# 272 further matmuls at the end of a two-layer decoder step

## The chip, the cores and the metric

The kernel runs on one core of a Trainium2 chip. The metric is the device time of the core in microseconds (us); the median of the runs counts. A profiled execution has a time of its own beside its span, which runs from the first to the last instruction that the profiler recorded. TensorE multiplies matrices (a weight load, then a matmul that streams columns past the weights), VectorE (DVE), ScalarE (ACT) and GpSimd (POOL) do the rest, and SyncE (SP) starts most transfers.

## The reference

The kernel computes one inference step of a hybrid causal decoder trunk with two layers, for 272 prompt tokens (16 of them learned) and 64 tokens of eight decoding sequences, 336 in all, 2048 channels wide. Cut to what matters here:

```python
def mixer_layer(x, ...):
    h = rms_norm(x, norm_g)
    z = h @ w_in                       # 2048 -> 8 * 2048
    u, pg, q, k, v, rg, gp, gr = jnp.split(z, IN_OFFSETS, axis=-1)
    ...
    merged = jax.nn.sigmoid(gp) * pool_branch + jax.nn.sigmoid(gr) * ret_branch
    return x + merged @ w_out, new_hist, S_new
...
y_prompt = rms_norm(xp, final_norm)[:, N_META:]
y_sample = rms_norm(xs, final_norm)
```

Nothing of this is changed. The further matmuls multiply parts of a table of cosines and sines that the kernel holds anyway, and no output depends on them.

## The kernel before

Channels lie on the partitions and tokens along the free axis, so each activation is a row of 16 tiles of 128 channels by 336 tokens (320 in the second layer from its output side on, where the 16 learned tokens are no longer needed). All weights pass through one stream of steps. A step loads a block of 512 by 256 weights (`dma_step`), splits it into a high and a low part in float32r (`split_step`, L159 on ScalarE and L165 on VectorE) and runs 24 matmuls on it (`main_step`): for each of four k-slices and two halves of 128 output channels, high by high, high by low and low by high, each with a weight load of 128 columns of its own. Every matmul of the kernel but the transposes goes through the helper `mm`, line 155, so rows of L155 are told apart by their tiles and widths. Work between the steps (retention, pooling, gates) hangs on step numbers (`at`) and uses four PSUM buffers of 512 columns in turn (`side`).

The program order is written out by hand: what stands later in the program comes later on its engine. After the last step, two small groups of matmuls make the token sums and spread the resulting scale over the partitions (`token_sums`, `spread_rstd`). VectorE scales the eight parts of the result (L880) with that scale, read from the PSUM buffer `last`, and each part is sent out as soon as it is scaled, by SyncE's queue and ScalarE's in turn (L881):

```python
    for i in range(8):
        xf = H["xf", i]
        nc.vector.tensor_tensor(out=xf[:, :, n], in0=xf[:, :, n], in1=bc(last[:, n]), op=ALU.mult)
        (nc.sync, nc.scalar)[i % 2].dma_start(out=o["yT"][i], in_=xf[:, :, n])
```

Then the pools are closed. Line 925 (the call that runs the program) stands for the drains and the semaphores of the common end.

Of the kernel before, what the change touches and what calls it, by code (L numbers as in the profile page):

```python
# [6 lines left out]
F32 = mybir.dt.float32  # L7
F32R = mybir.dt.float32r
# [26 lines left out]
C_ID, C_COS, C_SIN = 0, 128, 128 + T  # L35
# [42 lines left out]
def build(tc, a, o, g8):  # L78
    nc = tc.nc
# [23 lines left out]
    def open_pool(name, side=None, **kw):  # L103
        P[name] = tc.alloc_tile_pool(name=name, bufs=1, side=side, reuse_waits="tile", **kw)
        return P[name]

    def close_pool(name):
        P.pop(name).release()

    def bc(ap, n=2):  # L110
        return ap.unsqueeze(1).to_broadcast([128, n, ap.shape[-1]])
# [9 lines left out]
    def side():  # L121
        return sidep.tile([128, 512], F32, tag="side", bufs=4, name="side")
# [4 lines left out]
    cst = cp.tile([128, C_W], F32, name="cst")  # L127
# [26 lines left out]
    def mm(out, lhsT, rhs, start, stop):  # L154
        nc.tensor.matmul(out, lhsT, rhs, start=start, stop=stop)  # L155
# [722 lines left out]
    for i in range(8):  # L878
        xf = H["xf", i]
        nc.vector.tensor_tensor(out=xf[:, :, n], in0=xf[:, :, n], in1=bc(last[:, n]), op=ALU.mult)  # L880
        (nc.sync, nc.scalar)[i % 2].dma_start(out=o["yT"][i], in_=xf[:, :, n])  # L881
    for name in list(P)[::-1]:
        close_pool(name)

# [52 lines left out]
```

## Time and profile before

| what | value |
|---|---|
| median of two runs | 2845.77 us (2845.53 to 2846.01) |
| profiled execution, its own time | 2847.05 us |
| its span | 2845.3 us |
| mean granted clock of TensorE over the span | 0.997 |
| TensorE busy | 2821.2 us, 99% of the span |
| VectorE, ScalarE, GpSimd busy | 53%, 33%, 13% |

Busy time of TensorE comes from modelled ends of overlapping matmuls: the time from one matmul's start to the next one's start is shorter than the duration that a row gives, and it is the first that adds up to a stretch. The clock column tells the share of full speed that TensorE was granted: 1.00 is 2.4 GHz, 0.50 is 1.2 GHz.

### The profile page before, as it was taken

Reading aid. Unit: us, or ns where it says so; the run is one execution under the profiler, and the core shown is the slowest. Engines: PE = TensorE matmul, PEld = TensorE weight load, DVE = VectorE, ACT = ScalarE, POOL = GpSimd, SP = SyncE. Lnnn points to the kernel's source line nnn. Section 1 sums busy time; section 2 is a strip of 40 time slices with the busy share of each in tenths; the row PEclk is TensorE's granted clock in tenths of the full one; section 3 lists DMA queues with packets and bytes.
Section 4 is the critical chain, followed back from the end, with each engine's and each line's share of the span. In section 5 each row is a group of like instructions: output and inputs, shape, how many; then the busy total and the mean of one; then the engine's idle time right before and its main releaser. Section 6 shows DMA issues by size and latency. Waiting matters only on the chain.

```text
span 2845.3 us, 46391 instructions
## 1 busy us (share of the span) xinstructions
PE 2821.2 (99%) x19228; PEld 2796.1 (98%) x19228; DVE 1518.4 (53%) x1898; ACT 932.8 (33%) x1117; POOL 362.4 (13%) x560
## 2 busy tenths in 40 slices
PE   8999999999999999999999999999999999999997
PEld 8999999999999999999999999999999999999997
DVE  7655555544345664344455566655544465644543
ACT  4333333333223333333333333333342333333332
POOL 5222222210000000000112222222100000000000
PEclk9999999999999999999999999999999999999998
DMA  6556565654554444444555666666655544444443
GB/s 240 189 205 214 205 212 201 219 194 165 166 179 140 148 150 144 153 153 164 195 187 204 212 209 210 210 214 219 212 167 172 174 153 159 143 156 162 172 167 122
DMA packets 174259, 516.63 MB, mean 182 GB/s; under 512 B 23888, under 2 KB 46672, under 8 KB 174032
## 3 DMA queue, kind: packets, MB, share of 16 engines
q1 hardware_dynamic: 150976, 447.81, 46.2%
q0 software_dynamic: 21696, 63.99, 6.3%
q8 instruction: 150, 2.46, 0.3%
q10 hardware_dynamic: 1376, 1.87, 0.2%
q14 instruction: 61, 0.50, 0.1%
HBM read 447.91 MB, written 66.57 MB: 181 GB/s over the span
## 4 chain that ended last, share of the span: by engine, by line
PE 98%; issue 0%; DVE 0%; POOL 0%; POOLq 0%; ACT 0%; DVEq 0%; ACTq 0%
PE acc L155 91%; PE side L155 6%; PE side L314 1%; PE side L485 0%; DVE xf L880 0%; DVE h_lo L167 0%; POOLq L925 0%; POOL xsq L215 0%; POOL xsq L214 0%; DVE xs L780 0%; ACT sq L208 0%; DVEq L925 0%; DVE sinr L236 0%; POOLq L214 0%; ACTq L208 0%
## 5 line engine op out<-in xcount | busy, mean ns | idle before, releaser
L155 PE MATMUL acc<-act_hi,whi 128*128 128x320 f32 (+1 forms) x3328 | 1039.7, 312 | 0.0
L155 PE MATMUL acc<-act_lo,whi 128*128 128x320 f32 (+1 forms) x3328 | 1037.4, 312 | 0.0
L155 PE MATMUL acc<-act_hi,wlo 128*128 128x320 f32 (+1 forms) x3328 | 1036.3, 311 | 0.0
L165 DVE TENSOR_TENSOR wlo<-raw,whi 128x1024 fp32r<-128x1024 f32 x720 | 868.7, 1226 | 293.1 <-ACT whi L159 285.4
L159 ACT CAST whi<-raw 128x1024 fp32r<-128x1024 f32 x720 | 733.6, 1047 | 511.2 <-PE acc L155 406.6
L155 PE MATMUL acc<-h_lo,whi 128*128 128x336 f32 x2304 | 732.9, 318 | 5.0 <-DVE h_lo L167 5.0
L155 PE MATMUL acc<-h_hi,whi 128*128 128x336 f32 x2304 | 736.1, 319 | 1.4 <-ACT whi L159 1.4
L155 PE MATMUL acc<-h_hi,wlo 128*128 128x336 f32 x2304 | 730.5, 317 | 0.7 <-DVE wlo L165 0.7
L155 PEld LDWEIGHTS acc<-act_lo,whi 128*128 128x128 f32 x3328 | 626.5, 188 | 0.0
L155 PEld LDWEIGHTS acc<-act_hi,wlo 128*128 128x128 f32 x3328 | 625.1, 188 | 0.0
L155 PEld LDWEIGHTS acc<-act_hi,whi 128*128 128x128 f32 x3328 | 624.8, 188 | 0.0
L155 PEld LDWEIGHTS acc<-h_lo,whi 128*128 128x128 f32 x2304 | 436.6, 190 | 7.6 <-DVE h_lo L167 7.5
L155 PEld LDWEIGHTS acc<-h_hi,whi 128*128 128x128 f32 x2304 | 433.6, 188 | 1.6 <-ACT whi L159 1.6
L155 PEld LDWEIGHTS acc<-h_hi,wlo 128*128 128x128 f32 x2304 | 434.1, 188 | 1.0 <-DVE wlo L165 1.0
L418 DVE SCALAR_TENSOR_TENSOR sraw<-sraw,side 128x512 f32<-128x512 f32 x128 | 87.9, 686 | 175.5 <-PE side L155 175.5
L419 POOL DMA_DIRECT2D out_ret_s_dram<-sraw x128 | 71.4, 558 | 524.4 <-DVE sraw L418 518.3
L212 POOL TENSOR_TENSOR xsq<-sq 128x336 f32<-128x336 f32 (+1 forms) x3 | 2.8, 941 | 564.8 <-ACT sq L208 564.8
L161 ACT ACTIVATE kthi<-side,cst 128x256 fp32r<-128x256 f32 (+1 forms) x48 | 20.9, 468 | 136.6 <-PE side L314 136.6
L669 POOL DMA_DIRECT2D out_pool_u_dram<-uc x16 | 8.7, 545 | 440.5 <-DVE uc L624 440.5
L159 ACT CAST vthi<-side 128x256 fp32r<-128x256 f32 (+1 forms) x48 | 16.2, 371 | 146.2 <-PE side L314 146.2
L582 DVE SCALAR_TENSOR_TENSOR mb<-tr,acc 128x336 f32<-128x336 f32 (+1 forms) x32 | 14.4, 493 | 81.0 <-PE acc L155 81.0
L389 DVE TENSOR_TENSOR sc<-side,dtab 128x416 f32<-128x416 f32 (+1 forms) x16 | 9.3, 583 | 90.3 <-PE side L155 90.3
(152 smaller groups left out, 1862.1 us busy)
## 6 DMA issues: line engine op xcount, KB each, us to landing
raw<-in_w_in_dram SPq DMA_DIRECT2D x512, 512.0 KB, 4.3
sraw<-in_state_ret_dram SPq DMA_DIRECT2D x128, 256.0 KB, 4.2
out_ret_s_dram<-sraw POOLq DMA_DIRECT2D x128, 256.0 KB, 2.6
raw<-in_proj_ret_dram SPq DMA_DIRECT2D x64, 512.0 KB, 4.1
raw<-in_proj_pool_dram SPq DMA_DIRECT2D x64, 512.0 KB, 5.0
raw<-in_w_out_dram SPq DMA_DIRECT2D x64, 512.0 KB, 4.8
raw<-in_pool_w_dram SPq DMA_DIRECT2D x16, 512.0 KB, 3.3
kts<-ktd SPq DMA_DIRECT2D x16, 256.0 KB, 3.0
```

Of the source, the lines that this page charges most:

```text
L155: nc.tensor.matmul(out, lhsT, rhs, start=start, stop=stop)
L159: nc.scalar.copy(out=out, in_=in_)
L161: nc.scalar.activation(out=out, in_=in_, func=ACTF.Copy, scale=scale)
L165: nc.vector.tensor_tensor(out=out, in0=in_, in1=hi.bitcast(F32), op=ALU.subtract)
L212: eng.tensor_tensor(out=xsq[:, n], in0=sq[:, 0, n], in1=sq[:, 1, n], op=ALU.add)
L314: nc.tensor.transpose(ps[:rows, 128 * d:128 * d + 128], hs[src][:, d, 128 * b:128 * b + rows], ident)
L389: nc.vector.tensor_tensor(out=sc[:, w], in0=ps[:, w], in1=dtab[:, w], op=ALU.mult)
L418: nc.vector.scalar_tensor_tensor(out=s2, in0=s2, scalar=g8[h], in1=up, op0=ALU.mult, op1=ALU.add)
L419: nc.gpsimd.dma_start(out=o["ret_s"][l, b, h].rearrange("p (d e) -> p d e", d=2), in_=s)
L582: nc.vector.scalar_tensor_tensor(out=t[:, d, n], in0=H["tr", l, i][:, d, n], scalar=1.0, in1=acc[:, d, n], op0=ALU.add, op1=ALU.mult)
L669: nc.gpsimd.dma_start(out=o["pool_u"][l, 2 * g + i], in_=gs.pop(("uc", i)))
```

## The change

Behind the eight output transfers, a pool of its own holds a tile of 640 float32r columns (`p_m`) and one of 256 (`p_w`), both copied by ScalarE from the constants. Then TensorE runs 272 matmuls in groups of 8 (the first group has 16), each with its weight load, into four PSUM buffers, two in a row into the same one. Widths are 512 (16 + 8), 320 (64), 336 (64 + 56), 448, 384, 304, 312, 328 and 344 (8 each), and 320 with only 64 or 32 weight columns (8 each). The 320 and 336 wide ones step the start of the moving operand by 8 elements (32 bytes) from 0 to 56, and a series of 336 steps the start of the weights by the same amounts.

```diff
         (nc.sync, nc.scalar)[i % 2].dma_start(out=o["yT"][i], in_=xf[:, :, n])
+    pr = open_pool("probe", side="left")
+    pad = pr.tile([128, 8], F32, name="pad")
+    p_m = pr.tile([128, 640], F32R, name="p_m")
+    p_w = pr.tile([128, 256], F32R, name="p_w")
+    nc.gpsimd.memset(pad, 0.0)
+    nc.scalar.copy(out=p_m, in_=cst[:, C_COS:C_COS + 640])
+    nc.scalar.copy(out=p_w, in_=cst[:, C_COS:C_COS + 256])
+    ps = [side() for _ in range(4)]
+
+    def probe(cols, off=0, woff=0, wide=128, count=8):
+        for i in range(count):
+            mm(ps[i // 2 % 4][:wide, :cols], p_w[:, woff:woff + wide], p_m[:, off:off + cols], True, True)
+
+    probe(512, count=16)
+    for cols in (320, 336):
+        for off in range(0, 64, 8):
+            probe(cols, off)
+    for woff in range(8, 64, 8):
+        probe(336, 0, woff)
+    for cols in (512, 448, 384, 304, 312, 328, 344):
+        probe(cols)
+    for wide in (64, 32):
+        probe(320, wide=wide)
     for name in list(P)[::-1]:
         close_pool(name)
```

## Rows read from the trace of the kernel before

**Rows 1.** The page: engines' busy time, and shares of the chain that ended last.

```profile
PE 2821.2 (99%) x19228; PEld 2796.1 (98%) x19228; DVE 1518.4 (53%) x1898; ACT 932.8 (33%) x1117; POOL 362.4 (13%) x560
...
PE acc L155 91%; PE side L155 6%; PE side L314 1%; PE side L485 0%; DVE xf L880 0%; DVE h_lo L167 0%; POOLq L925 0%; POOL xsq L215 0%; POOL xsq L214 0%; DVE xs L780 0%; ACT sq L208 0%; DVEq L925 0%; DVE sinr L236 0%; POOLq L214 0%; ACTq L208 0%
```

**Rows 2.** Timeline of the last 20 us: start, us, engine, line, operation, tiles.

```profile
2826.33 0.30 PE L155 MATMUL acc<-act_hi,wlo 128*128 128x320 f32 x1
...
2832.53 0.69 PE L155 MATMUL side<-cst,cosr 64*128 64x64 f32 x2
...
2833.26 5.94 DVE L880 TENSOR_TENSOR xf<-xf,side 128x640 f32<-128x640 f32 x8 [1.74 <-PE side L155]
...
2834.84 4.93 ACTq L881 DMA_DIRECT2D out_yT_dram<-xf  x4
```

**Rows 3.** What SyncE waited for in the last 25 us: us, times, longest.

```profile
SPq L925 <- DMA out_yT_dram<-xf: 4.8, 2, 3.5
```

**Rows 4.** The end's own instructions on line 925: durations in ns, first and last start.

```profile
L925 SPq DRAIN  x3: 7/7/7, 2844.4 to 2844.8; - x3
...
L925 PEldq DRAIN  x2: 13/856/1698, 2831.6 to 2844.8; - x2
```

**Rows 5.** Busy time by stretch at the end: engines, granted clock, DMA share, GB/s.

```profile
2830.00:2830.50 0.50, 0.00 (x0) 0.00 (x0) 0.04 (x1) 0.00 (x0) 0.39 (x1) 1.00 0.00 0
2830.50:2831.00 0.50, 0.00 (x0) 0.00 (x0) 0.00 (x0) 0.00 (x0) 0.50 (x1) 0.56 0.00 0
...
2843.50:2844.00 0.50, 0.00 (x0) 0.00 (x0) 0.00 (x0) 0.00 (x0) 0.00 (x0) 0.50 0.00 0
```

**Rows 6.** ScalarE: one instruction of the timeline, two groups of the page.

```profile
2813.57 0.74 ACT L208 ACTIVATE sq<-xs 128x640 f32<-128x640 f32 x1 [6.99 <-DVE xs L780]
L159 ACT CAST whi<-raw 128x1024 fp32r<-128x1024 f32 x720 | 733.6, 1047 | 511.2 <-PE acc L155 406.6
L159 ACT CAST vthi<-side 128x256 fp32r<-128x256 f32 (+1 forms) x48 | 16.2, 371 | 146.2 <-PE side L314 146.2
```

**Rows 7.** TensorE's timeline in steady work, second layer, 320 columns.

```profile
2399.74 0.31 PE L155 MATMUL acc<-act_lo,whi 128*128 128x320 f32 x1
...
2402.37 0.31 PE L155 MATMUL acc<-act_lo,whi 128*128 128x320 f32 x1
```

**Rows 8.** The same in the first layer, 336 columns.

```profile
599.73 0.32 PE L155 MATMUL acc<-h_hi,wlo 128*128 128x336 f32 x1
...
602.36 0.32 PE L155 MATMUL acc<-h_lo,whi 128*128 128x336 f32 x1
```

**Rows 9.** The same between two steps: 272 columns, then 144.

```profile
74.91 0.29 PE L155 MATMUL side<-qhi,khi 128*128 128x272 f32 x1
...
75.53 0.28 PE L155 MATMUL side<-qhi,klo 128*128 128x272 f32 x1
...
75.83 0.28 PE L155 MATMUL side<-qhi,klo 128*128 128x144 f32 x1
...
76.17 0.27 PE L155 MATMUL side<-qhi,klo 128*128 128x144 f32 x1
```

**Rows 10.** TensorE's timeline near the start of the program, after a wait.

```profile
14.23 0.42 PE L155 MATMUL acc<-h_lo,whi 128*128 128x336 f32 x1 [2.18 <-DVE h_lo L167]
14.49 0.41 PE L155 MATMUL acc<-h_hi,wlo 128*128 128x336 f32 x1
14.69 0.48 PE L155 MATMUL acc<-h_hi,whi 128*128 128x336 f32 x1
...
17.21 0.48 PE L155 MATMUL acc<-h_hi,whi 128*128 128x336 f32 x1
18.73 0.42 PE L155 MATMUL acc<-h_lo,whi 128*128 128x336 f32 x1 [1.03 <-DVE h_lo L167]
18.99 0.31 PE L155 MATMUL acc<-h_hi,wlo 128*128 128x336 f32 x1
```

**Rows 11.** Busy time by stretch there: columns as in rows 5, PE first.

```profile
14.50:15.00 0.50, 0.50 (x4) 0.50 (x4) 0.50 (x1) 0.41 (x2) 0.43 (x1) 0.56 1.06 419
...
17.50:18.00 0.50, 0.20 (x1) 0.00 (x0) 0.50 (x1) 0.32 (x2) 0.50 (x1) 0.53 1.02 410
18.00:18.20 0.20, 0.00 (x0) 0.00 (x0) 0.20 (x1) 0.20 (x1) 0.20 (x1) 1.00 0.94 369
```

**Rows 12.** Groups by line: warm-up matmuls whose result nobody reads, and their weight loads.

```profile
L155 PE MATMUL side<-ones 128*128 128x128 f32 x24 | 4.5, 369 | 1.1 <-DVE ones L826 1.1
```

## The prediction

> **What bounds the kernel now.** I read the page first: the chain that ended last is TensorE's, 91% of it the main matmuls [rows 1], and TensorE is busy for 99% of the span [rows 1]. That says why the kernel takes 2846 us, but the change touches none of that: it stands behind the last output transfer. So the question is only what the end looks like, and I read the timeline of the last 20 us engine by engine. The dense matmuls stop at 2826.6; the small ones of the token sums and the spreading end at 2833.2; VectorE's eight scalings end at 2833.26 + 5.94 = 2839.20; ScalarE's four issues of output transfers end at 2834.84 + 4.93 = 2839.77 [rows 2]. From there on no engine computes. SyncE waits for the outputs to land, up to 3.5 us at a time [rows 3], its first drain stands at 2844.4 [rows 4], and the span ends at 2845.3: 0.9 us of common end behind the last wait. The end is bound by VectorE and then by the landing of the outputs, while TensorE has been drained since 2831.6 + 1.7 = 2833.3 [rows 4]. The reader is to see that TensorE, the bound of everything before, is free for the last 12 us, and that its clock is at 0.50 of full speed from 2830.7 on [rows 5].
>
> **Where the new work starts.** Nothing is removed. The 272 matmuls need `p_m` and `p_w`, which ScalarE copies, and these copies stand behind its four issues in the program; the last issue waits for VectorE's last scaling. So the copies can't begin before 2839.77. A 640 wide ScalarE instruction took 0.74 us; scaling the 1024 wide cast of 1.047 us by width gives 0.65, so 0.74 is the upper of two near values and I take it; the 256 wide cast took 0.37 [rows 6]. With some 0.05 us for the handover (an estimate from the gap between VectorE's start at 2833.26 and TensorE's end at 2833.22), TensorE starts at 2839.77 + 0.74 + 0.37 + 0.05 = 2840.93. Its other condition, that the four PSUM buffers are free, holds by then: the last to read one is VectorE, up to 2839.20. The memset on GpSimd is read by nobody, and that engine has nothing left; it costs nothing. Nothing waits behind the two copies but ScalarE's part of the common end.
>
> **What 272 matmuls take.** Durations in rows overlap, so I price from start to start. In steady work 18 steps of 320 columns take 2402.37 - 2399.74 = 2.63 us, 146.1 ns each [rows 7]; 17 steps of 336 columns take 2.63 us, 154.7 ns each [rows 8]; 5 steps of 272 take 0.62 us, 124 ns each [rows 9]. At full clock (2.4 GHz) the bare widths are 133.3, 140.0 and 113.3 ns, so what is left is 12.8, 14.7 and 10.7 ns: one column per cycle and about 13 ns for each pair of weight load and matmul. Weight loads don't bind at these widths: at 144 columns, where 128 weights take longer than the columns, the step is (76.17 - 75.83) / 3 = 113 ns [rows 9], below every width here. The sum:
> - 64 of 320 columns: 64 x 146.1 = 9.35 us.
> - 120 of 336: 120 x 154.7 = 18.56 us.
> - Widths that the trace lacks, as width / 2.4 + 13 ns: 304, 312, 328, 344, 384, 448 and 512 give 139.7, 143.0, 149.7, 156.3, 173.0, 199.7 and 226.3 ns, together 1188 ns, eight of each: 9.50 us. The first sixteen of 512: 3.62 us. Were the 13 ns to grow with the width (512 x 154.7 / 336 = 235.7 ns), the 24 of 512 would cost 0.2 us more.
> - 16 of 320 with 64 or 32 weight columns: between the bare 133.3 and the 146.1 of a full load, 2.1 to 2.3 us; I take 146.1, 2.34 us.
>
> Together 43.4 us for 95,168 columns. The bare columns alone are 39.7 us, and no row shows less, so the bound below is 3.7 us less.
>
> The Trainium skill ("TensorE: Matmul & The Clock Gate", section "Wait — 56ns, not 53.3ns?") puts the fixed part at 2.5 ns for each back-to-back matmul. By it the sum would be 40.3 us, some 3 us less. The rows, with a weight load for every matmul, show 10.7 to 14.7 ns, and the rows decide.
>
> **What the trace doesn't show: byte offsets.** In the kernel before, every moving operand and every weight slice of the main matmuls starts at a multiple of 64 bytes in its tile (by the widths in the code: 336 elements of 4 bytes are 21 x 64, 16 tokens are 64, a half of the weights 512). 112 of the new matmuls start their columns, and 56 their weights, 8 to 56 elements off. From below: nothing. From above, the dearest step at full clock in a stream of such matmuls is the one whose weight load was not prefetched, 18.99 - 18.73 = 0.26 us for 336 columns [rows 10], 0.105 us over the steady one; for 168 matmuls that is 17.6 us. I take nothing: an offset alters neither the columns nor the number of weights, and the nearest rows, the steady ones, lie at one end. Half of the doubt goes into the range.
>
> **The clock.** When TensorE starts again it has done nothing for 7.7 us and its clock has been at 0.50 (1.2 GHz) since 2830.7, some 4 us after the dense work stopped [rows 2, 5]. What happens then is shown once, near the start: after an idle 2.18 us the granted clock fell at about 14.7, matmuls of 336 columns went on at (17.21 - 14.69) / 9 = 280 ns [rows 10], that is the bare width at 1.2 GHz, and the clock was back at 18.0 [rows 11]. So 3.3 us of slow clock, with such matmuls through most of it, were enough. At 280 ns against 154.7, 45% of the slow time is lost. I take 3.5 us, a loss of 1.6 us. If it takes twice that, 3.1; if the clock rises at once, nothing.
>
> **The end.** The last matmul ends about 0.16 us later than its step (0.31 against 0.146) [rows 7]. The 0.9 us of common end come behind it instead of behind the landing. The outputs have landed by 2844.4 and lie fully beside the matmuls, so they leave the path; without that cover, if the new work took under 3.5 us, they would still set the end.
>
> **The sum.** 2840.93 + 43.4 + 1.6 + 0.16 + 0.9 = 2887.0 us of span. The profiled execution's own time is 2847.05 - 2845.3 = 1.75 us above its span, so 2888.7. It lies 1.28 us above the median of the runs, so the forecast in terms of the median is 2887.4 us, 41.7 us or 1.5% more. About 2% is what I count as distinguishable from no change here, that is 2902.7 us: the work is real, but it falls within that.
>
> **The rivals.**
> - The clock stays low. The gate that fell at 2830.7 might not rise again before the end. Every column then takes 280 / 336 = 0.833 ns, and 95,168 take 79.3 us in place of 43.4 + 1.6: 2887.4 + 34.3 = 2921.7 us, slower by 2.7%. For it: the start after a long pause, at half clock. Against it: the recovery [rows 10, 11] under the same kind of work. It decides from (2902.7 - 2887.4 + 1.6) / 0.45 = 38 us of slow clock on. 4 in 100.
> - Weight loads stop being prefetched, or unaligned starts cost as much. At the upper end of 0.105 us for the 168 offset matmuls it gives 2905.0 us, for all 272 it gives 2916.0. For it: no row has such offsets, and the same weights are loaded eight times over. Against it: in the rows a load for the next matmul always runs under the present one, whatever tile it is from. 4 in 100 (3 for the first, 1 for the second).
> - Repeats of the same weights are not loaded again, or the offsets help: down to the bare columns, 2887.4 - 3.7 = 2883.7. It lies in my range; the warm-up multiplies one tile by itself twelve times and stands with 24 matmul passes in the trace [rows 12], and the page counts as many weight loads as matmuls in all, 19,228 [rows 1].
> - The matmuls are not there at all, since nobody reads them: 2845.8 us plus at most the 1.1 us of copies, hidden under the landing. Against it: the unread warm-up ran [rows 12]. 2 in 100.
> - They start earlier than the program order says, beside the scalings, from 2833.3 on: 7.6 us less, 2879.8. Against it: ScalarE's queue shows its issues in program order and waiting for VectorE. 3 in 100.
>
> **How the numbers follow.** The forecast with its own variations has 87 in 100. Its range reaches below to the bare columns with a clock that is back at once, 2887.4 - 3.7 - 1.6 = 2882.1, which needs both, so I stop at 2883; above to the doubled slow time (1.5 us more) and half the doubt on offsets (8.8 us), together 2897.7, where I stop at 2897. The rivals outside hold 13 in 100, and the edges of the forecast's own spread the rest of the 2 in 10. Slower by over 2%: the low clock (4), the second rival for all 272 (1) and one for the unnamed, 6 in 100. Faster by over 2%: no case gives it, 1. Within 2%: 93.
>
> **What the new profile would show.** The first 512 wide matmul at about 2841, right behind two ScalarE copies that begin at 2839.8; a granted clock of 0.50 at first and 1.00 some 3 to 4 us later, with some eight matmuls of 0.43 us from start to start before it rises; then 146 ns at 320 columns and 155 at 336, the same at every offset; the output transfers where they were; the end 0.9 us behind the last matmul. All rows up to 2839 unchanged. What would make it wrong: a step that depends on the offset by tens of ns, a clock that stays at 0.50, a start before 2839.8, or PSUM writes that hold up wide matmuls.

## The result and the profile after

The changed kernel takes 2888.95 us (median of two, 2888.64 to 2889.27), 43.2 us or 1.52% more than before by the medians; the ratio estimated over the runs is 1.0148 with a 95% interval of 1.0131 to 1.0164. The forecast was 2887.4 us within 2883 to 2897. The profiled execution took 2889.27 us with a span of 2887.5 us. TensorE's matmul passes grow from 19,228 [rows 1] to 19,500, by the 272 that were added.

The end of the timeline of the changed kernel, which answers to [rows 2] (start, us, engine, line, operation, tiles, count, and in brackets the idle time before and what ended it). A merged row carries the width of its first matmul, so the last row holds all 272, whatever their width:

```profile
2832.43 5.94 DVE L880 TENSOR_TENSOR xf<-xf,side 128x640 f32<-128x640 f32 x8 [1.74 <-PE side L155]
2834.01 4.93 ACTq L881 DMA_DIRECT2D out_yT_dram<-xf  x4
2838.98 0.73 ACT L887 CAST p_m<-cst 128x640 fp32r<-128x640 f32 x1 [8.37 <-DVE xf L880]
2839.61 0.40 ACT L888 CAST p_w<-cst 128x256 fp32r<-128x256 f32 x1
2840.07 46.46 PE L155 MATMUL side<-p_m,p_w 128*128 128x512 f32 x272 [7.68 <-ACT p_w L888]
```

Read it from top to bottom: scalings, issues, copies, matmuls, each behind the one before. VectorE ends its scalings 0.8 us earlier than in the execution of before (2838.37 against 2839.20), which is how far two executions differ; so I compare distances from there. The first matmul starts 1.70 us later, the last ends 48.16 us later.

What SyncE waited for in the last 60 us, answering to [rows 3] (us, times, longest):

```profile
SPq L948 <- PE side L155: 43.0, 1, 43.0
SPq L881 <- DVE xf L880: 32.9, 4, 30.3
SPq L948 <- DMA out_yT_dram<-xf: 4.8, 2, 3.5
```

The landing of the outputs takes what it took before; behind it SyncE now waits 43.0 us for TensorE. That is the change in one line, and it agrees with the measured 43.2 within the scatter of the runs.

Busy time by stretch, answering to [rows 5] (stretch, its length, busy time of PE, PEld, DVE, ACT and POOL, granted clock, DMA share, GB/s):

```profile
2840.00:2845.50 5.50, 5.43 (x13) 4.28 (x14) 0.00 (x0) 0.01 (x1) 0.00 (x0) 0.50 0.36 125
2845.50:2846.00 0.50, 0.50 (x3) 0.40 (x2) 0.00 (x0) 0.00 (x0) 0.00 (x0) 0.50 0.00 0
2846.00:2847.00 1.00, 1.00 (x6) 0.86 (x6) 0.00 (x0) 0.00 (x0) 0.00 (x0) 0.95 0.00 0
```

The clock stands at 0.50 for 6.0 us of dense matmuls: it is back at 1.00 a tenth into the last stretch, at 2846.1.

The new matmuls by width (busy us for the group, mean ns of one, which overlaps with the next):

```profile
L155 PE MATMUL side<-p_m,p_w 128*128 128x336 f32 x120 | 18.6, 316 | 0.0
L155 PE MATMUL side<-p_m,p_w 128*128 128x320 f32 x64 | 9.5, 309 | 0.0
L155 PE MATMUL side<-p_m,p_w 128*128 128x512 f32 x24 | 8.7, 533 | 7.7 <-ACT p_w L888 7.7
```

And the timeline inside seven groups: 320 columns with a start of 0 and then of 56 elements (the first of the nine belongs to the group before), 336 columns with start 0, with start 56, and with weights starting at 56, and 320 columns with 64 and with 32 weight columns:

```profile
2846.76 1.19 PE L155 MATMUL side<-p_m,p_w 128*128 128x320 f32 x7
2854.68 1.49 PE L155 MATMUL side<-p_m,p_w 128*128 128x320 f32 x9
2856.16 1.24 PE L155 MATMUL side<-p_m,p_w 128*128 128x336 f32 x7
2864.77 1.24 PE L155 MATMUL side<-p_m,p_w 128*128 128x336 f32 x7
2873.38 1.24 PE L155 MATMUL side<-p_m,p_w 128*128 128x336 f32 x7
2884.03 1.33 PE L155 MATMUL side<-p_m,p_w 128*64 128x320 f32 x8
2885.20 1.33 PE L155 MATMUL side<-p_m,p_w 128*32 128x320 f32 x8
```

A merged row runs to the end of its last matmul, so a step is (us - mean of one) / (count - 1): (1.19 - 0.308) / 6 = 147 ns and (1.49 - 0.309) / 8 = 148 ns for 320, and (1.24 - 0.316) / 6 = 154 ns three times for 336. With 64 and with 32 weight columns it is (1.33 - 0.309) / 7 = 146 ns. Over all the groups of eight, the mean step from start to start lies between 146 and 147 ns at 320 and between 153 and 155 at 336: offsets by multiples of 32 bytes and the number of weight columns show nothing beyond that.

### The profile page after: what moved, and what is told of

Its sections match the earlier page's. It is cut to its first block, busy times and chain, and to the rows that moved or that the text cites. A ratio compares the mean times of both kernels' runs of the same rounds, so it can differ in the third digit from the quotient of the medians.

```text
span 2887.5 us, 46940 instructions
## 1 busy us (share of the span) xinstructions
PE 2867.9 (99%) x19500; PEld 2841.2 (98%) x19500; DVE 1518.2 (53%) x1898; ACT 935.6 (32%) x1119; POOL 363.8 (13%) x561
## 4 chain that ended last, share of the span: by engine, by line
PE 98%; issue 0%; DVE 0%; POOL 0%; ACT 0%; POOLq 0%; ACTq 0%; DVEq 0%
PE acc L155 90%; PE side L155 7%; PE side L314 1%; PE side L485 0%; DVE xf L880 0%; POOLq L948 0%; POOL xsq L214 0%; POOL xsq L215 0%; DVE xs L780 0%; ACT sq L208 0%; DVEq L948 0%; ACT p_m L887 0%; ACTq L881 0%; ACTq L948 0%; DVE sinr L236 0%
## 5 line engine op out<-in xcount | busy, mean ns | idle before, releaser
L367 POOL COPY qpad<-tmp 128x32 f32<-128x32 f32 x64 | 52.0, 842 | 42.1 <-DVE tmp L291 41.2
```

What stands on the lines that cost most here:

```text
L367: nc.gpsimd.tensor_copy(out=H["qpad"][:, d, 4 * half_:4 * half_ + 4, 8 * half_:8 * half_ + 8], in_=qr[:, d, b0_:b0_ + 32].rearrange("p (b ...
```

## The experiments

The theory at the outset was that of the prediction: the matmuls run one behind the other from ScalarE's copies on, each priced from start to start; offsets are free; the clock costs a little at the beginning. All experiments change only what stands behind the dense work, and the outputs are computed as before. Each ran with the kernel before on its chip, whose median there was 2847.17 us for the first four, 2847.61 for the next three and 2847.16 for the last four; differences are taken from that. Where tenths matter I read the trace, as the time from the end of VectorE's scalings to the end of the last matmul: 48.16 us in the changed kernel's own profile.

**Copies without matmuls.** The body of the probe is left out:

```diff
-    probe(512, count=16)
...
-        probe(320, wide=wide)
```

> The pool, the memset and the two ScalarE copies stay, the 272 matmuls go. If the matmuls alone make the added time and the copies lie under the landing of the outputs (copies end near 2840.9, the landing at 2844.4), the time is that of the kernel before, 2845.8 us within 0.6. If the pool or the copies themselves delay the end, behind their 1.1 us or more, it is 2846.9 us or later.

Measured 2847.73 us, ratio to before 1.0003 (0.9993 to 1.0012): no difference. ScalarE's timeline and, below it, SyncE's waits (us in total, times, longest) show the cover:

```profile
2839.50 0.72 ACT L887 CAST p_m<-cst 128x640 fp32r<-128x640 f32 x1 [8.37 <-DVE xf L880]
2840.13 0.40 ACT L888 CAST p_w<-cst 128x256 fp32r<-128x256 f32 x1
```

```profile
SPq L938 <- DMA out_yT_dram<-xf: 4.8, 2, 3.6
```

The copies end at 2840.5 while SyncE waits on for the outputs. The pool, the memset and the copies cost nothing that these runs can tell (0.6 us between the medians, inside the interval); the added time is the matmuls'.

**Copies first.** The pool and the two copies move ahead of the loop over the eight parts:

```diff
+    pr = open_pool("probe", side="left")
...
+    nc.scalar.copy(out=p_w, in_=cst[:, C_COS:C_COS + 256])
     for i in range(8):
         xf = H["xf", i]
```

> The two copies stand ahead of the eight scalings and output issues instead of behind them. If TensorE's start hangs on ScalarE's program order (the copies behind the last issue), it now starts right after its spreading matmuls, near 2833.3 instead of 2840.1 or so, and the time falls by about 6.5 us, to 2882.4 us. If what held the start was VectorE's last read of a PSUM buffer that the new matmuls write, only the first four matmuls get in earlier and the time falls by under 3 us, to 2886 us or more.

Measured 2885.93 us, 38.8 above before (ratio 1.0136, 1.0119 to 1.0153). The timeline of TensorE:

```profile
2831.80 2.93 PE L155 MATMUL side<-p_m,p_w 128*128 128x512 f32 x6
2837.99 43.87 PE L155 MATMUL side<-p_m,p_w 128*128 128x512 f32 x266 [3.27 <-DVE xf L887]
```

Neither expectation holds in full: not four but six matmuls got in early (two into each of three buffers), and then TensorE waited for VectorE, whose eight scalings, 5.94 us from 2831.91 on, read the fourth buffer. So the start has two conditions, one behind the other: ScalarE's order, and 1.7 us before it the buffer `last`. The prediction named both and priced the later. The last matmul ends 44.02 us behind the scalings, 4.1 less than in the changed kernel. That is all accounted for: the rest starts 0.15 us behind the scalings instead of 1.70, which gives 1.55, and six of the slow first matmuls (bare 512 columns at 1.2 GHz, 0.427 us each) are already done, which gives 2.6.

**Bfloat16 tiles.** The disputed part of the price, what a matmul takes above its bare columns:

```diff
-    p_m = pr.tile([128, 640], F32R, name="p_m")
-    p_w = pr.tile([128, 256], F32R, name="p_w")
+    p_m = pr.tile([128, 640], mybir.dt.bfloat16, name="p_m")
+    p_w = pr.tile([128, 256], mybir.dt.bfloat16, name="p_w")
```

> The tiles of the new matmuls are bfloat16 instead of float32r, all else equal. If what a matmul takes above its bare columns (about 13 ns at 320) belongs to the pair of weight load and matmul, the times stay: 146 ns at 320, 154 at 336, 2888.9 us within 0.6. If it belongs to streaming 4-byte columns (0.455 ns a column instead of 0.417), 320 columns fall to about 134 to 136 ns and 336 to 140 to 143, and the time falls by about 3.4 us to 2885.5.

Measured 2887.06 us, 39.9 above before (1.0138, 1.0123 to 1.0153). The widths again, and a stretch of the timeline:

```profile
L155 PE MATMUL side<-p_m,p_w 128*128 128x336 bf16 x120 | 17.3, 306 | 0.0
L155 PE MATMUL side<-p_m,p_w 128*128 128x320 bf16 x64 | 8.9, 299 | 0.0
```

```profile
2851.80 4.37 PE L155 MATMUL side<-p_m,p_w 128*128 128x320 bf16 x31
```

The step is (4.37 - 0.299) / 30 = 135.7 ns at 320 against 147, and the 120 of 336 take 17.3 us against 18.6. So "about 13 ns for each pair of weight load and matmul" is not a price of the pair: with the same pairs in bfloat16 it is 2.4 ns, and the rest goes with float32r. Whether that is the format itself or its four bytes per element, no run tells apart. The whole shrinks less than the 3.4 us expected, from 48.16 to 45.25 us behind the scalings, 2.9 us. The Trainium skill ("TensorE: Matmul & The Clock Gate", section "Wait — 56ns, not 53.3ns?") gives a fixed 2.5 ns per warm matmul; with bfloat16 the trace agrees with it, with float32r it shows five times as much at 320 columns.

**Kept warm.** 63 more matmuls, results not read, in TensorE's pauses at the end:

```diff
+    keep = side()
+    hi = H["merged", 1][0]
+
+    def bridge(count):
+        for _ in range(count):
+            mm(keep[:, 0:320], hi[:, 0, 16:144], hi[:, 1, 16:336], True, True)
+
+    bridge(12)
     token_sums(YBLOCKS)
+    bridge(7)
     n = slice(NM, T)
     last = spread_rstd(YBLOCKS, False)
+    bridge(44)
```

> 63 matmuls of 320 columns on held data, results not read, fill TensorE's pauses before the new work: 12 behind the dense work, 7 behind the token sums, 44 behind the spreading (44 x 0.146 = 6.4 of 7.7 us). If the slow first stretch comes from the pause, the granted clock stays at 1.00, the first sixteen of 512 take 3.7 us instead of 6.5, and the time falls by 2.9 us to 2886.0. If the clock falls all the same, the 44 take 11.8 us at 1.2 GHz, run past 2840 and the time rises by about 3 us, to 2892.

Measured 2886.91 us, 39.7 above before (1.0139, 1.0123 to 1.0154). Busy time by stretch:

```profile
2834.00:2838.00 4.00, 4.00 (x30) 4.00 (x29) 4.00 (x6) 0.00 (x0) 0.00 (x0) 1.00 0.89 309
2838.00:2840.00 2.00, 1.00 (x7) 0.74 (x6) 0.33 (x1) 1.03 (x2) 0.00 (x0) 1.00 1.03 358
2840.00:2844.00 4.00, 3.97 (x18) 3.32 (x19) 0.00 (x0) 0.00 (x0) 0.00 (x0) 1.00 0.49 169
```

The clock stays at 1.00 and the new matmuls run at full clock from their first one. From the end of the scalings (2838.33) to the last matmul's end (2883.70) it is 45.37 us, 2.8 less than in the changed kernel; 2.9 was expected. So the slow first stretch comes from TensorE's pauses behind the dense work, and they are worth 2.8 us against this profile of the changed kernel (2.0 against its second one, in the last experiment). Which pause does it isn't told apart here. It isn't the longest alone: the clock had fallen before that one began [rows 5], and the run with three buffers below, which has no such pause, starts at 0.50 too.

**All 512 wide.** `probe(512, count=272)` is all that runs.

> All 272 new matmuls are 512 wide. The prediction priced a width as its bare columns plus 13 ns: 226.3 ns at 512. The rival, read from the new trace (137.4 ns at 304, 231.4 at 512), is a rate of 0.455 ns a column: 233.0 ns. After some 15 matmuls at 1.2 GHz (6.4 us as in the changed kernel), 257 steps take 58.2 us by the first and 59.9 by the second: 2907.4 us against 2909.1 us.

Measured 2907.82 us, 60.2 above before (1.0214, 1.0198 to 1.0229). In the timeline 222 of them in a row:

```profile
2849.78 50.48 PE L155 MATMUL side<-p_m,p_w 128*128 128x512 f32 x222
```

The step, which decides here rather than the total, is (50.48 - 0.389) / 221 = 226.7 ns: the bare 213.3 plus 13.3, the prediction's price and not the rate's 233.0. Yet in the changed kernel, the eight of 512 between other widths took 232 ns (seven in 1.78 us: (1.78 - 0.390) / 6):

```profile
2874.68 1.78 PE L155 MATMUL side<-p_m,p_w 128*128 128x512 f32 x7
```

That they stand between other widths doesn't explain it. In the next experiment the same eight stand in the same place, and only the starts of the matmuls before them differ; there they take (1.75 - 0.389) / 6 = 227 ns:

```profile
2874.43 1.75 PE L155 MATMUL side<-p_m,p_w 128*128 128x512 f32 x7
```

**Single-element offsets.** `range(0, 64, 8)` becomes `range(8)`, `range(8, 64, 8)` becomes `range(1, 8)`.

> The starts of the moving operand and of the weights step by single elements (4 bytes, 0 to 28) instead of by 8 elements (32 bytes, 0 to 224). If a start off a line of the memory costs nothing, as the steps of 32 bytes cost nothing, the time is that of the changed kernel, 2888.9 us within 0.6. If a start that is no multiple of 32 bytes makes TensorE read one more piece per matmul, the 168 offset ones take longer: at 10 ns each 1.7 us more, and the groups differ in the trace.

Measured 2888.94 us, 41.3 above before (1.0147, 1.0132 to 1.0162). The changed kernel was 43.2 above its before in the first pair and 42.2 in the last experiment, so the medians show no added time; in the trace the last matmul ends 47.98 us behind the scalings, against 48.16 and 47.36. The timeline for 320 columns with start 0 and start 5, and 336 columns with start 0 and with start 5 (a row may reach one matmul into the next group):

```profile
2846.59 1.19 PE L155 MATMUL side<-p_m,p_w 128*128 128x320 f32 x7
2852.47 1.21 PE L155 MATMUL side<-p_m,p_w 128*128 128x320 f32 x7
2855.89 1.08 PE L155 MATMUL side<-p_m,p_w 128*128 128x336 f32 x6
2861.88 1.26 PE L155 MATMUL side<-p_m,p_w 128*128 128x336 f32 x7
```

Steps of 147, 150, 153 and 157 ns. The dearest start costs 3 to 4 ns. The other starts show less: over all 64 of 320 columns the mean step is 147.2 ns against 146.6 in the changed kernel, over all 120 of 336 it is 153.9 against 153.7, under 0.1 us in all. Starts that are no multiple of 32 bytes are all but free too; the 10 ns of the rival are not there.

**Narrow.** `probe(160, wide=32, count=272)` is all that runs.

> All 272 new matmuls are 160 wide with 32 weight columns, where bare columns plus 13 ns and a rate per column lie furthest apart in relation: 79.7 ns against 72.8. With 6.2 us at 1.2 GHz first (46 matmuls of 133 ns), the other 226 take 18.0 us by the first, 16.5 by the second: 2866.6 us against 2865.1. If the load of 32 weights has a price of its own that shows at this width, the steps are longer than 80 ns.

Measured 2865.96 us, 18.4 above before (1.0067, 1.0050 to 1.0084). The timeline:

```profile
2849.81 12.41 PE L155 MATMUL side<-p_m,p_w 128*32 128x160 f32 x167
```

The step is (12.41 - 0.238) / 166 = 73.3 ns, the rate's 72.8 and not the fixed price's 79.7. With the run of 512 columns the two have now each lost once: what float32r costs grows with the width, but not evenly.

**Three buffers.** As with the copies first, and `ps` holds three buffers, `ps[i // 2 % 3]`.

> As with the copies first, and the new matmuls use three PSUM buffers in turn instead of four, so that the one that VectorE still reads is not among them. If ScalarE's order and that buffer were the two conditions of the start, all 272 now run without a pause from the spreading matmuls on, beside the scalings and the transfers: some 8.2 us less than the changed kernel, about 2880.7 us. If matmuls that run beside them slow the scalings or the transfers, VectorE's eight take longer than 5.94 us, and if a third condition holds the start, the time stays near that of the copies-first kernel, 4 us less.

Measured 2880.08 us, 32.9 above before (1.0118, 1.0101 to 1.0135) and 9.3 below the changed kernel on the same chip (the last experiment). TensorE and VectorE:

```profile
2832.11 45.06 PE L155 MATMUL side<-p_m,p_w 128*128 128x512 f32 x272
...
2832.22 5.94 DVE L887 TENSOR_TENSOR xf<-xf,side 128x640 f32<-128x640 f32 x8 [1.74 <-PE side L155]
```

All 272 run through without a pause, from 6.04 us before the end of the scalings instead of 1.70 behind it, and the scalings take 5.94 us as ever. SyncE's wait for the outputs is that of [rows 3] too:

```profile
SPq L948 <- DMA out_yT_dram<-xf: 4.8, 2, 3.5
```

There is no third condition, and running beside them slows neither the scalings nor the transfers. The last matmul ends 39.0 us behind the scalings, 9.1 less than in the changed kernel: 7.7 from the start, 1.4 from 45.06 us of matmuls instead of 46.46, because the clock was back after 3.1 us here (at 2835.2).

**The ladder, in float32r and in bfloat16.** 24 matmuls of 512, then 24 each of ten widths with 32 weight columns:

```diff
-    probe(512, count=16)
...
+    probe(512, count=24)
+    for cols in (128, 160, 192, 224, 256, 288, 352, 416, 480, 512):
+        probe(cols, wide=32, count=24)
```

> The new matmuls, still float32r, are 24 of 512 and then 24 each of 128, 160, 192, 224, 256, 288, 352, 416, 480 and 512 columns with 32 weight columns, to see how the time above the bare columns grows. A fixed 13 ns gives 66.3 ns at 128, 93 at 192, 133 at 288, 160 at 352, 213 at 480. A rate of 0.456 ns a column gives 58.3, 87.5, 131.3, 160.4 and 218.7. A surplus that grows with the width and stops at 13.3 ns (0.0417 ns a column up to 320) gives 58.7, 88, 132, 160 and 213.3. The totals lie within 0.6 us of each other, near 2884 us; the steps in the trace decide.

> The same ladder with bfloat16 tiles. If the time above the bare columns comes from float32r, every width takes its bare columns plus 2.5 ns (55.8 ns at 128, 82.5 at 192, 122.5 at 288, 149.2 at 352, 202.5 at 480), and the time is 2.2 us below the float32r ladder. If it comes from the PSUM side or the pairing with weight loads at some widths, the two ladders show the same steps there.

Measured 2884.87 us in float32r (37.7 above before; 1.0135, 1.0120 to 1.0151) and 2881.57 in bfloat16 (34.4 above; 1.0122, 1.0107 to 1.0137). Timelines inside the groups of 128, 256, 480 and 512, float32r first:

```profile
2852.41 1.18 PE L155 MATMUL side<-p_m,p_w 128*32 128x128 f32 x17
2860.15 2.43 PE L155 MATMUL side<-p_m,p_w 128*32 128x256 f32 x20
2874.79 4.43 PE L155 MATMUL side<-p_m,p_w 128*32 128x480 f32 x20
2879.72 5.03 PE L155 MATMUL side<-p_m,p_w 128*32 128x512 f32 x21
```

```profile
2847.79 1.11 PE L155 MATMUL side<-p_m,p_w 128*32 128x128 bf16 x17
2855.12 2.35 PE L155 MATMUL side<-p_m,p_w 128*32 128x256 bf16 x20
2868.76 4.21 PE L155 MATMUL side<-p_m,p_w 128*32 128x480 bf16 x20
2873.66 4.48 PE L155 MATMUL side<-p_m,p_w 128*32 128x512 bf16 x20
```

With the mean of one taken off (0.224, 0.276, 0.376, 0.391 us in float32r; 0.219, 0.272, 0.366, 0.379 in bfloat16) the steps are 60, 113, 213 and 232 ns against 56, 109, 202 and 216. Bfloat16 takes its bare columns (53.3, 106.7, 200.0, 213.3) plus 2.3 to 2.7 ns at these four widths, as expected; the totals lie 3.3 us apart where 2.2 were expected. Float32r takes 6 to 7 ns above them at 128 and 256, 13 at 480 and 19 at 512, where the same width took 13.3 in a run of its own. Between them, the mean steps are 73.6, 88.4, 103.3, 130.9, 159.9 and 188.5 ns at 160, 192, 224, 288, 352 and 416. All three forms that the expectation named fail somewhere. The fixed 13 ns is over 6 ns off at 128, and the rate of 0.456 ns a column 5 ns off at 480. The surplus that grows and stops at 13.3 ns meets eight of the ten widths within 2 ns and misses 256 by 4 and 512 by 5. Steps lie 6 to 13% above the bare columns, and none of the three is a law.

**The changed kernel again**, unchanged, beside the last three.

> The changed kernel itself beside the others on one chip. The same theory as before holds: 43.2 us above the kernel before within 0.8, by 42.8 us of matmuls at full clock behind 1.7 us from the last scaling to the start, and 2 to 3 us lost to the slow clock, whose length in the trace is expected between 4.5 and 6.5 us.

Measured 2889.36 us, 42.2 above before (1.0150, 1.0135 to 1.0165). That is 1.0 below the 43.2 of the first pair, just outside the 0.8 that I gave it, and its slow stretch was shorter than expected: the matmuls start at 2842.82 and the clock is back at about 2847.1, 4.3 us later.

```profile
2846.50:2847.00 0.50, 0.50 (x3) 0.41 (x2) 0.00 (x0) 0.00 (x0) 0.00 (x0) 0.50 0.00 0
2847.00:2847.50 0.50, 0.50 (x4) 0.42 (x3) 0.00 (x0) 0.00 (x0) 0.00 (x0) 0.92 0.00 0
```

Its matmuls take 45.66 us in all, 0.8 less than in the first profile: the clock's share differs from one execution to the next, and the steps at full clock are the same in both. At full clock they come to 43.5 us as before, not the 42.8 expected. The shorter slow stretch does not explain the 1.0 us between the two medians, since this profiled execution was the slowest of its four (2891.21 us); that difference lies within the scatter of the runs (2845.8 to 2847.4 before, 2888.3 to 2891.2 changed).

## Why the prediction was right

- **The start: right.** 1.73 us behind the scalings was forecast, 1.70 measured, with copies of 0.73 and 0.40 us against 0.74 and 0.37. That it hangs on ScalarE's program order is shown by moving the copies; that the PSUM buffer is the next condition, by the three buffers. The rival of an earlier start is out for the changed kernel, and its price of 7.6 us was about what it is worth when both conditions are lifted (7.7).
- **The matmuls: right in sum.** 46.46 us, less the 2.8 that the clock cost and the 0.16 of the last one's tail, leave 43.5 against 43.4. The widths that the rows showed came out as they stood there (147 and 154 ns). The step that split off "about 13 ns for each pair of weight load and matmul" gave numbers within 6 ns for widths from 304 to 512. Near the rows, up to 344, that was to be expected; at 384 to 512 it was in part luck, for the reading was wrong: bfloat16 pairs show some 2.5 ns, float32r matmuls of 128 columns 7, and those of 512 13 in one run and 19 in another. At 128 columns it would have given 66.3 ns where 60 were measured.
- **Offsets and weight loads: right.** With 32 and 64 weight columns the step at 320 columns was that of 128, so no weight load set a step there. The reading that the load sets the 113 ns at 144 columns [rows 9] is borne out: with 32 weight columns, 160 columns took 73 ns. Nothing was taken and nothing beyond 1 to 2 ns is seen at steps of 32 bytes; single-element steps show 3 to 4 ns at the worst start. The 17.6 us of the upper bound was far too wide: its step of 0.26 us is that of the first matmul behind a wait [rows 10], and no offset matmul showed it.
- **The clock: right mechanism, size too small.** The forecast took 3.5 us of slow clock from its one example near the start of the program and lost 1.6 us; the changed kernel's profile has 6.0 us, with thirteen full steps at the slow clock instead of some eight, and keeping TensorE busy through the pauses gives 2.8 back. This is the term that was mis-sized, by 1.2 us. The doubled stretch that the range allowed for covers it. Starts behind the same pause in this study had 4.3 us (the changed kernel again) to 6.0 us of slow clock; the start without that pause (three buffers) had 3.1. The rival of a clock that stays low needed 38 us and is out.
- **The end: right.** The span ends 1.0 us behind the last matmul (2887.5 against 2840.07 + 46.46 = 2886.53), 0.9 was forecast; the outputs land under the matmuls, and the copies alone cost nothing. That the matmuls might be dropped is out by their count.
- **The total: close, in part by luck.** The forecast of 2887.4 us missed the median by 1.55 us, but the span by only 0.5 (2887.0 against 2887.5): the clock's 1.2, and 0.1 each for the matmuls and the end, are more, and 0.8 is less because the work up to the last scaling ended earlier in this execution. The other 1.0 us comes from turning a profile into a median: the profiled execution of before lay 1.28 us above its median, that of the changed kernel 0.32. Measured again, the added time was 42.2 us, 0.5 above the 41.7 of the forecast.

## What to carry to other kernels

Work that is added behind the last result is paid from start to start, not by the durations in a row, and its price is best taken from rows of the same type and of widths nearby; a constant split off from two near widths is not a law. Look for all the conditions of a start, not only the one that ends last: lifting the first here uncovered a PSUM buffer, and both had to go for 9 us. After a pause of TensorE, price the slow stretch as a range, since the same program showed 6.0 us in one execution and 4.3 in another.

## What the runs showed that was not expected

- Bfloat16 matmuls take their bare columns at 2.4 GHz plus 2.3 to 2.7 ns at each width that was read, from 128 to 512. Float32r matmuls take 6 to 19 ns more than bare, and the same 512 columns, with the same operands and starts, took 226.7 ns in a run of equals, 232 between other widths, and 227 between the same other widths when only the starts of earlier matmuls differed. What makes the difference was not found; the load of the weights is not it at 320 columns, which took the same 146 ns with 32, 64 and 128 weight columns.
- TensorE's clock can go up and down again within one tail. With the copies first it was granted 0.50 when they began at 2831.8, 1.00 from 2834.9 when six matmuls had run, 0.50 from 2838.3 after a wait of 3.3 us with the new stream already going, and 1.00 from 2841.7:

```profile
2831.80:2834.80 3.00, 2.93 (x7) 1.82 (x6) 2.89 (x4) 0.00 (x0) 0.00 (x0) 0.50 0.25 89
2834.90:2838.20 3.30, 0.21 (x1) 0.24 (x2) 2.94 (x5) 0.00 (x0) 0.00 (x0) 1.00 1.02 356
2838.30:2841.60 3.30, 3.30 (x9) 2.60 (x8) 0.00 (x0) 0.00 (x0) 0.00 (x0) 0.50 0.95 332
2841.70:2845.00 3.30, 3.30 (x23) 3.24 (x22) 0.00 (x0) 0.00 (x0) 0.00 (x0) 1.00 0.01 3
```
